# Linear attention in a two-layer trunk: the gate projection r as four pairs in seven block products, and head outputs with tokens on partitions

## The chip, the cores and the metric

The kernel runs on one core of one Trainium2 chip. The metric is the device time of one execution in microseconds, the median of the runs shown. Matrix products run on TensorE (PE in the profile, its weight loads PEld), elementwise work on VectorE (DVE) and ScalarE (ACT), and POOL (GpSimd) issues the DMAs that add into their destination. SP issues nearly all other loads.

## The reference

The program is a trunk of two layers over 512 tokens of width 1024, all in float32. Layer 0 mixes by pooling and short convolution, layer 1 by gated linear attention (GLA); each is followed by a gated ConvFFN of width 2816. The change lies in layer 1's mixer, which reads the normed input hn = rmsnorm(x) through one projection, split into q, k (512 columns each), v, r (1024 each) and a gate of rank 16:

```python
q, k, v, r, gl = jnp.split(hn @ gla_w_in, ...)
g = jax.nn.log_sigmoid(gl @ w_g2 + b_g) / 16
# four heads, chunks of 64 tokens; bcum = cumsum of g in a chunk
att = where(mask, (q * exp(bcum)) @ (k * exp(-bcum)).T, 0)
o = att @ v + (q * exp(bcum)) @ state
state = exp(b_last) * state + (k * exp(b_last - bcum)).T @ v
o = o * lax.rsqrt(jnp.mean(o * o, axis=-1, keepdims=True) + EPS) * norm_g   # per head, 256 wide
y = (o * silu(r)) @ gla_w_out
```

## The kernel before

Activations lie with channels on partitions: a tile is 128 channels by 512 tokens. The input norm is put off: the projections work on x times the norm's gain, and their results are multiplied afterwards by rs, the factor per token spread over the partitions (y4 holds the same factors with tokens on partitions). For precision every product is done in three: weights and activations are each split into a high and a low part (`hi` is a copy on ScalarE in the rounded format fp32r, `lo` the difference, on VectorE), and hi x hi, hi x lo and lo x hi are summed in PSUM. Products of the attention itself run in plain fp32.

The q/k projection of a head is not done as two plain tiles but as one pair of tiles in seven block products, a scheme of Strassen's kind: of the 2 x 2 blocks of weights (left and right tile, two halves of the contraction) and of activations (`mixed`, sums of x's halves in tokens and channels), seven products of half width, 12 matmuls of 256 columns each, stand for eight. `seven_weights` makes the sums of weights: `load_sum` loads two quarters, `add_sum` adds two others to them by a DMA on POOL's queue (the tile s31), `load_left` and `load_right` bring three quarters of the rest, and `s2_sum` and `s4_sum` form the other sums on VectorE; all are then split in high and low (L484, L490). `keep`, `add_p5` and the last sum put the result together from the banks stx, styz and stz.

The r projection is eight plain tiles, `gate(i)`: 24 matmuls of 512 columns each (L1324), scaled by rs (L370), then Silu. Their weights come through the same queue of blocks as the plain tiles of other stages, `weight_order`, with one load (L218) and one split (L223, L227) a tile.

A head goes through `keys` and `keys2` (q and k times the decays), `scores` (att, and the transposes kot of the keys), `kv`, `states`, and `outputs`. `outputs` makes o with channels on partitions: two banks of 128 channels by 512 tokens, 14 matmuls with 128 result columns. The norm of o is then a sum over partitions: squares on ScalarE (L1215), added, split, and summed by two matmuls with ones (`totals`, L315 and L316, the tile ss), followed by the chain of `norm_wide` on 128x512 tiles; `scale` multiplies o by the result ro and the norm's gain (L1235), and `out_gate` by silu(r), and splits the product into y_h and y_l for the output projection `go`.

From layer 1's projection to the end of the r tiles each step has a planned time by hand: `at(t, fn)` puts a step at t, `then(us, fn)` also moves t on by what TensorE needs, and `run_plan` sorts all steps by time and fixes that order on PE, DVE and ACT. An engine works through its own list in that order; a step that has to wait holds up those behind it on its engine. DMA queues likewise issue in order. Banks of PSUM (eight) and tiles of SBUF come from pools, and a new user waits for the old one's last reader.

The order of the attention stage is written out: r tile, q/k pair, r tile, q/k pair and so on, the steps of the heads set in between, and from the fifth r tile on r alone. Ahead of it, the value and gate projection runs in four blocks of columns (vg), with the gate's logits (`gate_logits`, the tile z) of heads 0 and 1 after the second block and of heads 2 and 3 within the third.

Of the kernel before, what the change touches and what calls it, by code (L numbers as in the profile page):

```python
# [73 lines left out]
def trunk_kernel(ctx, tc, xT, cols, w_ab, w_pool, w_abo, w_vg, w_qk, w_r, w_g2, w_go, w_up, w_dn, w_ds, outT):  # L74
# [109 lines left out]
    def weight_order():  # L184
# [7 lines left out]
        for l in range(2):  # L192
            for j, k0, kt in down_blocks():
                yield w_dn[l, j, :, k0 * P : (k0 + kt) * P], kt, P, SKEW * (l == 1 and j == KD - 1)
            if l == 0:
                off = 0
                for n, ks in zip(VG_COLS, VG_K):
                    for kt in ks:
                        yield w_vg[:, off : off + kt * n], kt, n, VG_SKEW
                        off += kt * n  # L200
                for i in range(8):
                    yield w_r[i], KD, P
                for j in TILE_ORDER:
                    yield w_go[j], KD, P
# [251 lines left out]
    def seven_weights(src, base, pool, sums, behind=False, lead=None, later=0.0):  # L456
# [50 lines left out]
        at(base - 26.0, queued_sum if behind else load_sum)  # L507
        at(base - 20.0, add_sum)
# [12 lines left out]
        at(base - (18.0 if lead == 0 else 15.4), load_left)  # L521
        at(base - (13.0 if lead == 0 else 9.7), load_right)
        for n, (t, step) in enumerate(zip(when, steps)):
            at(base + t + ((0, 0, 1.2, 1.2, 0.6, 0.6)[lead or 0] if 3 <= n <= 6 else later if n == 0 else 0.0), step)
# [510 lines left out]
    y4 = sp.tile([P, NTT], F32, tag="y4", name="y4")  # L1035
    rs = slot(name="rs")
# [159 lines left out]
    def outputs(h):  # L1196
        q = heads[h]
        att = att_t[h % 2]
        q["o"] = []
        for e in range(2):  # L1200
            o = bank("o")
            for p in range(NTT):
                cs = slice(p * P, (p + 1) * P)
                PE.matmul(o[:, cs], vcols(p, h * 256 + e * P, P), att[:, cs], start=True, stop=p == 0)
                if p:
                    PE.matmul(o[:, cs], q["st"][p][:, e * P : (e + 1) * P], q["q2"][:, cs], start=False, stop=True)
            q["o"].append(o)

    def squares_of(h, t):
        q = heads[h]  # L1210

        def raw():
            q["sq"] = [slot(name="osq") for _ in range(2)]
            for sq, o in zip(q["sq"], q["o"]):
                S.activation(sq, o, AF.Square)  # L1215

        def total():
            V.tensor_tensor(q["sq"][0], q["sq"][0], q["sq"][1], ALU.add)
            q["ro"], q["norm"] = norm_wide(q["sq"][0], 256, "ro")

        at(t, raw)
        at(t + (0.6 if h == 3 else 1.3), total)
        ready_at = (6.5, 6.5, 1.7, 0.8)[h]
        at(t + ready_at, lambda: q["norm"][0]())
        at(t + ready_at + (1.6 if h < 2 else 0.6), lambda: q["norm"][1]())

    def out_norm(h, t):
        q = heads[h]
        late = 13.0 if h == 0 else 0.0
        for step, after in zip(range(3, 8), (0.0, 0.7, 1.4, 2.2, 3.0 + late)):  # L1230
            at(t + after, lambda step=step: q["norm"][step]())

        def scale(e):
            q.setdefault("y", []).append(slot(name="y"))
            V.scalar_tensor_tensor(q["y"][e], q["o"][e], col("gnorm", e), q["ro"], ALU.mult, ALU.mult)  # L1235

        for e in range(2):
            at(t + 3.8 + late + 0.7 * e, lambda e=e: scale(e))

    def out_gate(h, e, t):  # L1240
        i = 2 * h + e

        def gate():
            y = heads[h]["y"][e]
            V.tensor_tensor(y, y, sil[i], ALU.mult)

        def high():
            y_h[i] = slot(F32R, "yh")
            S.activation(y_h[i], heads[h]["y"][e], AF.Copy)

        def low():
            y_l[i] = slot(F32R, "yl")
            V.tensor_tensor(y_l[i], heads[h]["y"][e], f32(y_h[i]), ALU.subtract)
# [33 lines left out]
    for b, (n, ks) in enumerate(zip(VG_COLS, VG_K)):  # L1287
        k0 = 0
        for i, kt in enumerate(ks):
# [14 lines left out]
            if b == 2 and i == 0:  # L1304
                for h in range(HEADS):
                    at(t + 2.2 + 0.1 * h, lambda h=h: log_gate(h))
                    at(t + 4.6 + 0.1 * h, lambda h=h: log_gate2(h))
                    if h < 2:
                        at(t + 6.0 + 2.0 * h, lambda h=h: log_gate3(h))
# [3 lines left out]
    scaled_at, sil_at = {}, {}  # L1313

    def project_into(name, key, store, between, split_at):
        q = {}

        def part(i):
            if i == 0:
                q["o"] = (bank(name), *ready.pop(0))  # L1320
            o, h, lo = q["o"]
            w, a = ((h, xh), (h, xl), (lo, xh))[i // 2]
            for k in (k1, k2)[i % 2]:
                PE.matmul(o, w[:, k, :], a[k], start=i == 0 and k == 0, stop=k == KD - 1 and i == 5, skip_group_check=True)  # L1324

        def out():
            store(key, scaled(q["o"][0], rs, name))

        next_block(13.0, *split_at)
        for i in range(6):  # L1330
            then(HK * MM, lambda i=i: part(i))
            if i in between:
                between[i]()
        at(t + (-0.8 if key == 7 else 0.3), out)

    qk_ops = {}

    def queries_keys(h):
        nonlocal t
        w = seven_weights(w_qk[h], t, "gla", 2)  # L1340
        b, q = {}, {}

        def product(name):
            if not qk_ops:
                qk_ops.update(operands(mixed))
# [5 lines left out]
            seven_product(w, b, qk_ops, name, out, first, ts)  # L1351
# [13 lines left out]
        def query():  # L1365
            V.tensor_tensor(q["q"], b["yz"], q["q"], ALU.add)

        def query2():
            V.tensor_tensor(q["q"], q["q"], rs, ALU.mult)
            heads[h]["q"] = q["q"]  # L1370

        for n, name in enumerate(DOWN_SEVEN):
            at(t + n * UNIT, lambda name=name: product(name))
        at(t + 1 * UNIT + 0.1, lambda: keep("q", lo_t))
        at(t + 3 * UNIT + 0.1, lambda: keep("q", hi_t))
        at(t + 4 * UNIT + 0.2, lambda: add_p5("q"))
        at(t + 5 * UNIT + 0.1, lambda: keep("k", hi_t))
        at(t + 5 * UNIT + 0.6, lambda: add_p5("k"))
        t += 7 * UNIT
        at(t - 0.6, query)  # L1380
        at(t + 0.1, lambda: keep("k", lo_t))
        at(t + 0.15, query2)
        at(t + 0.8, key)

    def store_r(i, u):
        sil[i] = u

    def gate(i, between={}, split_at=(6.0, 4.8)):
        project_into("r", i, store_r, between, split_at)
        at(t + 1.2, lambda: S.activation(sil[i], sil[i], AF.Silu))  # L1390
        sil_at[i] = t + 1.8
# [201 lines left out]
```

## Time and profile before

| | |
|---|---|
| median of 3 runs | 1006.9 us (1006.19, 1006.9, 1437.49) |
| profiled execution: span, first to last instruction | 1005.9 us |
| profiled execution's time by the median: span and what lies around it | 1005.9 + 1.0 us |
| TensorE busy in the span | 995.5 us (99%) |
| VectorE, ScalarE, POOL busy | 851.1 (85%), 616.1 (61%), 81.3 (8%) us |
| TensorE in the chain that ended last | 90% |
| attention stage, from the first r matmul to the first matmul of `go` | 513.84 to 625.07 us |
| HBM read | 145.35 MB, 147 GB/s over the span |

The page's first part is busy time by engine, the fourth the chain of work that ended last, followed back from the end. A matmul's busy time runs from its start to its modelled end, so matmuls that follow each other overlap: the distance between starts tells the pace, and the chain gives it. A group's row shows count, busy time, mean ns of one, and the idle time before them with what ended it.

### The profile page before, as it was taken

To read this page: it belongs to the slowest core of one execution; us is meant where nothing else is said; L and a number is where in the kernel's file an instruction comes from. 1 tells how busy PE (TensorE), PEld (TensorE's weight loads), DVE (VectorE), ACT (ScalarE), POOL (GpSimd) and SP (SyncE) were. 2 spreads that over 40 slices of the span, in tenths; PEclk is the share of its full clock that TensorE was granted. 3 is DMA by queue.
4 is the path that set the end of the run, shared out by engine and by line. 5 is a ranking of instruction groups with operands and counts; after the bars stand their busy time and mean duration, and the time that the engine had idled before them with its cause. 6 is when DMAs were issued, how large, how long until landed. Compare 5 with 4: busy or idle time off the path is not lost.

```text
span 1005.9 us, 17757 instructions
## 1 busy us (share of the span) xinstructions
PE 995.5 (99%) x7070; PEld 927.9 (92%) x7070; DVE 851.1 (85%) x1241; ACT 616.1 (61%) x959; POOL 81.3 (8%) x105
## 2 busy tenths in 40 slices
PE   9999999999999999999999999999999999999996
PEld 7888889999999988899999998889999999988896
DVE  7886689999999997768768787889999999997775
ACT  6442467667666754345775777667676676754451
POOL 0000211111111000002000000111101101000000
PEclk9999999999999999999999999999999999999998
DMA  6533757788787454527325122677888777454522
GB/s 220 154 102 105 179 125 171 207 201 196 197 205 189 128 127 136 137 81 206 99 82 140 53 75 87 183 170 167 211 209 197 187 204 190 130 124 141 128 85 84
DMA packets 64083, 151.22 MB, mean 150 GB/s; under 512 B 5408, under 2 KB 8352, under 8 KB 64000
## 3 DMA queue, kind: packets, MB, share of 16 engines
q1 hardware_dynamic: 46640, 117.46, 37.7%
q0 software_dynamic: 16672, 31.99, 19.2%
q8 instruction: 55, 0.90, 0.4%
q10 hardware_dynamic: 688, 0.65, 0.2%
q14 instruction: 28, 0.23, 0.1%
HBM read 145.35 MB, written 2.10 MB: 147 GB/s over the span
## 4 chain that ended last, share of the span: by engine, by line
PE 90%; DVE 4%; ACT 2%; DMA 2%; issue 1%; DVEq 0%; ACTq 0%
PE stx L538 28%; PE styz L538 16%; PE dn L268 15%; PE go L268 4%; PE abo L268 4%; PE r L1324 3%; PE pc L268 2%; PE dn L538 2%; PE pb L268 2%; PE px L268 2%; PE stz L538 2%; PE vg L1112 1%; PE vg L1113 1%; PE vg L1114 1%; PE pu L268 1%
## 5 line engine op out<-in xcount | busy, mean ns | idle before, releaser
L490 DVE TENSOR_TENSOR lo<-raw,hi 128x1024 fp32r<-128x1024 f32 x112 | 136.7, 1220 | 14.1 <-ACT hi L484 13.8
L484 ACT ACTIVATE hi<-raw 128x1024 fp32r<-128x1024 f32 x112 | 117.8, 1057 | 31.9 <-DMA raw<-in_w_up 10.7
L227 DVE TENSOR_TENSOR lo<-raw,hi 128x1024 fp32r<-128x1024 f32 (+3 forms) x79 | 91.1, 1154 | 18.1 <-ACT hi L223 17.9
L466 POOL DMA_DIRECT2D s<-in_w_up x44 | 53.1, 1206 | 533.8 <-ACT yh L177 97.8
L223 ACT ACTIVATE hi<-raw 128x1024 fp32r<-128x1024 f32 (+3 forms) x79 | 78.7, 997 | 13.0 <-issue 3.9
L359 DVE SCALAR_TENSOR_TENSOR cacc<-u,colt,cacc 128x511 f32<-128x511 f32 x96 | 71.5, 744 | 3.9 <-ACT cacc L356 3.8
L356 ACT ACTIVATE cacc<-u,colt 128x512 f32<-128x512 f32 x48 | 39.2, 817 | 49.8 <-DVE u L660 40.2
L490 DVE TENSOR_TENSOR lo<-s,hi 128x1024 fp32r<-128x1024 f32 x56 | 68.2, 1217 | 0.0
L538 PE MATMUL stx<-th,hi 128*128 128x256 f32 x384 | 59.6, 277 | 0.2 <-ACT kk L645 0.2
L484 ACT ACTIVATE hi<-s 128x1024 fp32r<-128x1024 f32 x56 | 59.0, 1053 | 0.8
L538 PE MATMUL stx<-tl,hi 128*128 128x256 f32 x384 | 59.2, 276 | 0.0
L538 PE MATMUL stx<-th,lo 128*128 128x256 f32 x384 | 59.2, 276 | 0.0
L538 PE MATMUL styz<-xh,hi 128*128 128x256 f32 x368 | 56.9, 277 | 0.0
L538 PE MATMUL styz<-xh,lo 128*128 128x256 f32 x368 | 56.7, 276 | 0.0
L538 PE MATMUL styz<-xl,hi 128*128 128x256 f32 x368 | 56.7, 276 | 0.0
L268 PE MATMUL dn<-mh,hi 128*128 128x512 f32 (+1 forms) x238 | 56.5, 377 | 0.0
L268 PE MATMUL dn<-mh,lo 128*128 128x512 f32 (+1 forms) x238 | 56.4, 376 | 0.0
L268 PE MATMUL dn<-ml,hi 128*128 128x512 f32 (+1 forms) x238 | 56.4, 376 | 0.0
L538 PEld LDWEIGHTS stx<-th,hi 128*128 128x128 f32 x384 | 50.7, 188 | 0.7 <-ACT kk L645 0.4
L538 PEld LDWEIGHTS stx<-tl,hi 128*128 128x128 f32 x384 | 50.7, 188 | 0.0
L538 PEld LDWEIGHTS stx<-th,lo 128*128 128x128 f32 x384 | 50.7, 188 | 0.0
L268 PEld LDWEIGHTS dn<-mh,lo 128*128 128x128 f32 x238 | 42.9, 188 | 8.2
(334 smaller groups left out, 2583.2 us busy)
## 6 DMA issues: line engine op xcount, KB each, us to landing
s<-in_w_up SPq DMA_DIRECT2D x44, 512.0 KB, 6.9
s<-in_w_up POOLq DMA_DIRECT2D x44, 512.0 KB, 7.2
raw<-in_w_up SPq DMA_DIRECT2D x44, 512.0 KB, 6.7
raw<-in_w_dn SPq DMA_DIRECT2D x32, 448.0 KB, 3.4
raw<-in_w_up SPq DMA_DIRECT2D x44, 256.0 KB, 3.4
raw<-in_w_ab SPq DMA_DIRECT2D x14, 512.0 KB, 3.7
raw<-in_w_abo SPq DMA_DIRECT2D x8, 512.0 KB, 3.6
s<-in_w_ds SPq DMA_DIRECT2D x8, 512.0 KB, 6.5
```

The costliest lines, as they stand in the source:

```text
L223: S.activation(parts[0], raw, AF.Copy)
L227: V.tensor_tensor(parts[1], raw, f32(parts[0]), ALU.subtract)
L268: PE.matmul(out, w[:, k, :], a[k], start=first and i == 0 and k == 0, stop=last and i == 2 and k == n - 1, skip_group_check=loose,)
L356: S.activation(acc[0], u, AF.Identity, bias=col(bname, j), scale=col(wname, 2 * nj + j))
L359: V.scalar_tensor_tensor(a, u[:, : T - i], col(wname, (2 - i) * nj + j), a, ALU.mult, ALU.add)
L466: G.dma_start(w["s31"].rearrange("p (a n) -> p a n", a=2), part, accum_op=ALU.add)
L484: S.activation(h, src(), AF.Copy)
L490: V.tensor_tensor(lo, src(), f32(h), ALU.subtract)
L538: PE.matmul(b[out][:, ts], wt[:, ks[k]], a[k], start=first and i == 0 and k == 0, stop=i == 2 and k == HK - 1, skip_group_check=True,)
L1112: PE.matmul(o[c][:, :n], xh[kk][:, cs], h[:, k, :], start=kk == 0, stop=False)
L1113: PE.matmul(o[c][:, :n], xl[kk][:, cs], h[:, k, :], start=False, stop=False)
L1324: PE.matmul(o, w[:, k, :], a[k], start=i == 0 and k == 0, stop=k == KD - 1 and i == 5, skip_group_check=True)
```

## The change

The r projection is done in four pairs of tiles in seven block products, by the same code as q and k (`pair` takes the place of `queries_keys`, and of `gate` with `project_into`). The four q/k pairs now stand first, one after the other, and the four r pairs behind them, with the steps of the heads in between. The weights of r are laid out in pairs in memory.

A head's output is made with tokens on partitions: four pieces of 128 tokens by 256 channels, seven matmuls, with the roles of weights and data exchanged. Its mean square is then a sum along the row, which ScalarE's Square gives beside its result (`accum_out`); the root is taken on 128x4 tiles, ScalarE scales the pieces, and eight transposes on TensorE (`rows`) bring them back to channels on partitions for the gating, which now reads the bank directly.

q and k are no longer multiplied by rs: k's factor, with its sign, is put into v (y4n = -y4 * y4), and q's into the norm of the output. All four heads' gate logits stand after vg's second block, and the steps that follow them stand earlier. `seven_weights` can start loads (`begin`) and splits (`early`) at other times.

```diff
-                for i in range(8):
-                    yield w_r[i], KD, P
...
-    def seven_weights(src, base, pool, sums, behind=False, lead=None, later=0.0):
+    def seven_weights(src, base, pool, sums, behind=False, lead=None, later=0.0, begin=(26.0, 20.0, 15.4, 9.7), early=0.0):
...
-        at(base - 26.0, queued_sum if behind else load_sum)
-        at(base - 20.0, add_sum)
+        at(base - begin[0], queued_sum if behind else load_sum)
+        at(base - begin[1], add_sum)
...
         if pool == "gla":
-            when = (*when[:7], 4.4, 1.5, 5.3)
+            when = (-6.75, -4.35, -2.1, -1.6, -0.9, -0.2, 0.5, 4.4, 1.5, 5.3)
...
     def v_out(b, n, c):
         o = v_banks[b][c]
-        S.activation(vcols(c, b * 256, 256), o[:, :256], AF.Copy, scale=y4[:, c : c + 1])
+        S.activation(vcols(c, b * 256, 256), o[:, :256], AF.Copy, scale=y4n[:, c : c + 1])
...
     def outputs(h):
         q = heads[h]
         att = att_t[h % 2]
-        q["o"] = []
+        two = [bank("o") for _ in range(2)]
+        q["o"] = [two[p // 2][:, p % 2 * 256 : p % 2 * 256 + 256] for p in range(NTT)]
+        for p in range(NTT):
+            cs = slice(p * P, (p + 1) * P)
+            PE.matmul(q["o"][p], att[:, cs], vcols(p, h * 256, 256), start=True, stop=p == 0)
+            if p:
+                PE.matmul(q["o"][p], q["q2"][:, cs], q["st"][p], start=False, stop=True)
+
+    def out_norm(h, t, root=2.2):
+        q = heads[h]
+        small = {}
+
+        def squares():
+            two = [slot(name="ot") for _ in range(2)]
+            q["ot"] = [two[p // 2][:, p % 2 * 256 : p % 2 * 256 + 256] for p in range(NTT)]
+            small["s"] = sp.tile([P, NTT], F32, tag="os", name="os")
+            for p in range(NTT):
+                S.activation(
+                    q["ot"][p], q["o"][p], AF.Square, scale=y4[:, p : p + 1], accum_out=small["s"][:, p : p + 1]
+                )
+
+        def mean():
+            small["v"] = sp.tile([P, NTT], F32, tag="v4", name="v")
+            V.tensor_scalar(small["v"], small["s"], 1.0 / 256, EPS, ALU.mult, ALU.add)
+
+        def seed():
+            small["y"] = sp.tile([P, NTT], F32, tag="oy", name="oy")
+            S.activation(small["y"], small["s"], AF.Abs_reciprocal_sqrt, bias=eps_t, scale=1.0 / 256)
+
+        def factor():
+            r = sp.tile([P, NTT], F32, tag="t4", name="t")
+            f = q["f"] = sp.tile([P, NTT], F32, tag="of", name="of")
+            V.tensor_tensor(r, small["y"], small["v"], ALU.mult)
+            V.scalar_tensor_tensor(r, r, -0.5, small["y"], ALU.mult, ALU.mult)
+            V.scalar_tensor_tensor(r, r, 1.5, small["y"], ALU.add, ALU.mult)
+            V.tensor_tensor(f, r, y4, ALU.mult)
+
+        def scale():
+            for p in range(NTT):
+                S.activation(q["ot"][p], q["o"][p], AF.Copy, scale=q["f"][:, p : p + 1])
...
+    def rows(h):
+        q = heads[h]
+        q["yt"] = [bank("yt") for _ in range(2)]
         for e in range(2):
-            o = bank("o")
             for p in range(NTT):
-                cs = slice(p * P, (p + 1) * P)
-                PE.matmul(o[:, cs], vcols(p, h * 256 + e * P, P), att[:, cs], start=True, stop=p == 0)
-                if p:
-                    PE.matmul(o[:, cs], q["st"][p][:, e * P : (e + 1) * P], q["q2"][:, cs], start=False, stop=True)
-            q["o"].append(o)
-
-    def squares_of(h, t):
...
+                PE.transpose(q["yt"][e][:, p * P : (p + 1) * P], q["ot"][p][:, e * P : (e + 1) * P], ident)
...
         def gate():
-            y = heads[h]["y"][e]
-            V.tensor_tensor(y, y, sil[i], ALU.mult)
+            V.scalar_tensor_tensor(sil[i], heads[h]["yt"][e], col("gnorm", e), sil[i], ALU.mult, ALU.mult)
...
                 then(0.9, lambda: rsqrt_small(y4, sums(acc)[:, :NTT], NTT, D))
+                at(t + 2.0, lambda: V.scalar_tensor_tensor(y4n, y4, -1.0, y4, ALU.mult, ALU.mult))
...
-            if (b, i) in ((1, 1), (2, 0)):
-                for h in ((0, 1) if b == 1 else (2, 3)):
+            if (b, i) == (1, 1):
+                for h in range(HEADS):
                     then(0.24, lambda h=h: gate_logits(h))
                     at(t + 1.5, lambda h=h: gate_sizes(h))
...
+                    at(t + 3.4 - 0.1 * h, lambda h=h: log_gate(h))
+                    at(t + 5.8 - 0.1 * h, lambda h=h: log_gate2(h))
+                for h in range(3):
+                    at(t + 7.2 + 2.2 * h, lambda h=h: log_gate3(h))
...
-    def queries_keys(h):
+    def pair(src, kind, h, between=None, early=0.0, begin=(26.0, 20.0, 15.4, 9.7)):
...
-        def key():
-            V.scalar_tensor_tensor(q["k"], q["k"], -1.0, rs, ALU.mult, ALU.mult)
...
-        def query2():
-            V.tensor_tensor(q["q"], q["q"], rs, ALU.mult)
...
+        def left_scaled():
+            V.tensor_tensor(q["r"], q["r"], rs, ALU.mult)
+
+        def right_scaled():
+            V.scalar_tensor_tensor(q["n"], q["n"], -1.0, rs, ALU.mult, ALU.mult)
+
+        def silu(i, tile):
+            sil[2 * h + i] = q[tile]
+            S.activation(q[tile], q[tile], AF.Silu)
...
-    gate(0)
-    gates_of(0, t)
-    at(t + 4.9, lambda: log_gate3(2))
-    queries_keys(0)
-    head_keys(0, 1.6)
-    gate(1, {4: lambda: head_scores(0)}, (3.6, 2.4))
...
-    gate(5, {4: lambda: (head_kv(3), head_norm(2))})
-    gate(6, {1: lambda: head_out(3)})
-    gate(7, {1: lambda: head_norm(3)}, (10.0, 8.6))
...
+    pair(w_qk, "qk", 0)
+    head_keys(0, 0.2)
+    gates_of(1, t - 4.0)
+    at(t + 4.0, lambda: log_gate3(3))
+    pair(w_qk, "qk", 1)
+    head_keys(1, 0.2)
+    gates_of(2, t - 3.0)
+    head_scores(0)
+    pair(w_qk, "qk", 2, {3: (lambda: head_kv(0),)}, 1.6, (17.5, 12.5, 13.5, 9.0))
+    head_keys(2, 0.2)
+    gates_of(3, t - 5.0)
+    head_out(0, 4.5)
+    head_scores(1)
+    pair(w_qk, "qk", 3, {3: (lambda: head_kv(1),)}, 4.6)
+    head_keys(3, 0.2)
+    head_out(1)
+    head_scores(2)
+    pair(w_r, "r", 0, {3: (lambda: head_kv(2),)}, 4.6)
+    head_out(2)
+    head_scores(3)
+    pair(w_r, "r", 1, {3: (lambda: head_kv(3),), 5: (lambda: head_rows(0),)}, 4.6)
+    head_gates(0, -1.0)
+    head_out(3, 5.5)
+    pair(w_r, "r", 2, {3: (lambda: head_rows(1),)}, 2.5)
+    head_gates(1, -1.0)
+    pair(w_r, "r", 3, {2: (lambda: head_rows(2),), 5: (lambda: head_rows(3),)}, 0.0, (17.5, 12.5, 13.5, 9.0))
+    head_gates(2, -1.0)
+    head_gates(3, 3.0)
     for i in range(2):
-        block(t - 9.5 + 2.5 * i, t - 6.5 + 2.0 * i, t - 4.8 + 2.0 * i)
+        block(t - 9.5 + 2.5 * i, t - 4.5 + 2.0 * i, t - 2.8 + 2.0 * i)
...
-        "w_r": _blocks(gw[:, 2048:3072], P),
+        "w_r": _blocks(gw[:, 2048:3072], P).reshape(HEADS, 2, P, D).transpose(0, 2, 1, 3).reshape(HEADS, P, 2 * D),
```

More of the change, by code (lines that the diff above doesn't have):

```diff
@@ L1035, in trunk_kernel @@
     y4 = sp.tile([P, NTT], F32, tag="y4", name="y4")
+    y4n = sp.tile([P, NTT], F32, tag="y4n", name="y4n", bufs=1)
     rs = slot(name="rs")
@@ L1209, in squares_of @@
-    def squares_of(h, t):
[L1210 to L1238, printed above, removed]
+                PE.transpose(q["yt"][e][:, p * P : (p + 1) * P], q["ot"][p][:, e * P : (e + 1) * P], ident)
@@ L1310, in trunk_kernel @@
         for c in range(NTT):
             at(t + 0.1 + 0.4 * c, lambda b=b, n=n, c=c: v_out(b, n, c))
[L1313 to L1334, printed above, removed]
@@ L1350, in product @@
             }[name]
-            seven_product(w, b, qk_ops, name, out, first, ts)
+            seven_product(w, b, pair_ops, name, out, first, ts)
         def keep(tile, ts):
@@ L1374, in queries_keys, with left_sum @@
[L1374 to L1391, printed above, removed]
+        def left_sum():
+            V.tensor_tensor(q[left], b["yz"], q[left], ALU.add)
+            if kind == "qk":
+                heads[h]["q"] = q["q"]
@@ new lines, in right_done @@
+        def right_done():
+            heads[h]["k"] = q["k"]
+        def left_scaled():
[5 more added lines that the diff above has]
+            S.activation(q[tile], q[tile], AF.Silu)
+        for n, name in enumerate(DOWN_SEVEN):
+            for step in (between or {}).get(n, ()):
+                step()
+            starts_at.append(t)
+            then(UNIT, lambda name=name: product(name))
@@ L1393, in head_keys @@
     def head_keys(h, d=0.0):
         at(t + d, lambda: keys(h))
-        at(t + d + 2.6, lambda: keys2(h))
+        at(t + d + 2.4, lambda: keys2(h))
     def head_scores(h):
@@ L1402, in head_kv, with head_out, head_rows @@
     def head_kv(h):
-        then(1.0, lambda: kv(h))
+        then(1.3, lambda: kv(h))
         at(t + 0.1, lambda: states(h))
-    def head_out(h):
-        then(3.1, lambda: outputs(h))
-        squares_of(h, t + 0.1)
-    def head_norm(h):
-        then(0.46, lambda: heads[h]["norm"][2]())
-        out_norm(h, t + 0.1)
-        scaled_at[h] = t + 5.4
+    def head_out(h, root=2.2):
+        then(3.0, lambda: outputs(h))
+        out_norm(h, t + 0.1, root)
+    def head_rows(h):
+        then(0.9, lambda: rows(h))
     def gates_of(h, t):
```

75 lines of the change are left out of this document (34 added, 41 removed).

## The prediction, written before the changed kernel ran

> **What bounds the kernel now.** I read the page first: who is busy, and on which engine the chain that ended last lies.
>
> ```profile
> span 1005.9 us, 17757 instructions
> PE 995.5 (99%) x7070; PEld 927.9 (92%) x7070; DVE 851.1 (85%) x1241; ACT 616.1 (61%) x959; POOL 81.3 (8%) x105
> PE 90%; DVE 4%; ACT 2%; DMA 2%; issue 1%; DVEq 0%; ACTq 0%
> ```
>
> TensorE bounds it, but a "busy" PE here holds the time in which a matmul stood waiting too, so 99% is no proof of pace. Next the busy time of the attention stage, cut where the chain changes tiles: from the end of the value and gate projection (vg) to the first matmul of the output projection (go). The columns are the stretch, its length, the busy time of TensorE, its weight loads, VectorE, ScalarE and POOL with instruction counts, granted clock, DMA share and GB/s.
>
> ```profile
> 513.84:625.07 111.23, 110.97 (x749) 101.30 (x749) 88.01 (x147) 76.16 (x113) 2.44 (x2) 1.00 0.31 88
> ```
>
> The change lies here: 111.23 us, clock 1.00, VectorE 79% and ScalarE 68% busy, the DMA engines 31%. Pace is read from the chain in order of time, whose second column is how long a run of matmuls held the array.
>
> ```profile
> 513.84 5.45 PE r L1324 x24
> 519.29 1.38 PE stx L538 x12
> ...
> 528.83 4.56 PE r L1324 x20
> 533.38 0.89 PE att L1159 x8
> 534.27 0.84 PE att L1163 x8
> 535.12 0.34 PE kot L1167 x3
> ...
> 546.01 1.29 PE kv L1184 x6
> 547.30 4.58 PE r L1324 x20
> 551.88 0.44 PE o L1204 x4
> ...
> 555.01 0.89 PE att L1159 x8
> ...
> 567.78 0.23 PE ss L315
> 568.01 0.23 PE ss L316
> ...
> 620.88 0.50 PE ss L316
> 621.38 3.69 PE r L1324 x16
> 625.07 4.99 PE go L268 x22
> ```
>
> A plain r tile takes 5.45; a q/k pair in seven products 528.83 - 519.29 = 9.54; scores of a head 0.89 + 0.84 + 0.34 = 2.07; kv 1.29; a head's output 555.01 - 551.88 = 3.13; the two matmuls that sum its squares 0.46. The stage holds 8 x 5.45 + 4 x (9.54 + 2.07 + 1.29 + 3.13 + 0.46) = 43.60 + 65.96 = 109.56 us of work. It lasts 625.07 - 513.84 = 111.23, so 1.67 us of stall is all that better hiding could give; the rest must come from doing less on TensorE.
>
> **The change part by part, TensorE first.** Four r pairs in seven products replace eight plain tiles: they run the same loop on the same shapes as the q/k pairs, so 4 x 9.54 = 38.16 for 43.60: -5.44. The two matmuls of the squares go, 4 x 0.46: -1.84. A head's output is now seven matmuls with a 128x256 result and 128 rows of contraction, which is the shape of kv (three logical ones in 1.29, 0.43 each): 3.01 for 3.13, over four heads -0.48. New are eight 128x128 transposes a head, as in kot (three in 0.34, 0.113 each): 0.91, over four heads +3.63. The sum is -4.13, nearly all on the bounding engine.
>
> The transposes are the one price with two readings, for the group row gives each a far longer duration than its share of the chain:
>
> ```profile
> L1167 PE MATMUL kot<-ident,kb 128*128 128x128 f32 x12 | 2.0, 275 | 0.0
> ```
>
> 275 ns is start to end of one, 113 the distance between two that stand behind each other. Eight stand in a row in the new code, more than the three of kot, so I take 113; the other end is 275, which adds 32 x 0.162 = 5.2. The Trainium skill (TensorE: Matmul & The Clock Gate, Part 4: PE-mode transpose) speaks against the change here: in its words the clock gate's full rate "doesn't engage" for transposes, and it measured about 275 ns for one in a kernel. By that figure, an estimate from the page, the sum would be some 5 us worse. The trace agrees with its 275 as a duration, but shows a granted clock of 1.00 in this stage and the shorter distance.
>
> **Stalls.** Of the old ones the rows show the norm's at the end (ss at 620.88 took 0.50 for its 0.23); that chain goes. Between a head's keys and its scores lay part of a plain tile, 4.56, and now lies a whole pair, 9.54. So I drop the 1.67, and look for new ones. Three places can stall anew.
>
> First, all four gate-logit matmuls (z) stand together in the vg stage, and the next vg block takes its four banks from them, each when VectorE has read it:
>
> ```profile
> 491.12 0.47 PE z L1058 x2
> 491.39 1.41 DVE L1060 TENSOR_SCALAR z<-z,colt 128x512 f32<-128x512 f32 x2 [1.35 <-PE z L1058]
> ```
>
> One z is read 0.27 + 0.70 = 0.97 after its start; TensorE is through all four after 0.94. The later banks are asked for 12 matmuls apart, a quarter of the 5.5 that four such runs take (a vg block has as many columns as an r tile, 5.45), and two 128x512 passes (0.68 each, by the L1245 row below) stand between the second and third read: third bank free 0.27 + 3 x 0.70 + 1.36 = 3.73 after the first start, asked for at 0.94 + 0.3 + 2 x 1.36 = 4.0. 0.3 us of stall; 0 to 1.4, if those passes came first.
>
> Second, the weights of r. A plain tile needed one load and one split; a pair needs two loads, a sum made by a load and an adding DMA on POOL's queue, three wide splits and one narrow one. By the landings in this stretch:
>
> ```profile
> s<-in_w_qk SPq DMA_DIRECT2D x4, 512.0 KB, 5.2
> s<-in_w_qk POOLq DMA_DIRECT2D x4, 512.0 KB, 9.0
> ```
>
> load, then add: 5.2 + 9.0 = 14.2 us. The plan starts them 26 us ahead of most pairs, but 17.5 ahead of the third q/k pair and the last r pair; there the sum is first used some 5 us into the pair, after 2.3 of splitting, so 17.5 + 2.7 = 20.2 are there. SP issues in order, and each load waits for a buffer of three; a pair's last split is 6.5 us after its start, and the load that waits for it is planned after that. POOL has only these adds in the stage. I cost this at nothing; it is covered by 6 us, and without the cover costs what is missing, twice. Moved bytes rise by 4 x (1.75 - 1.0) = 3 MB, under a DMA share of 0.31.
>
> Third, the end: go's first part reads all of heads 0 to 2, and head 2's last split waits on ScalarE behind the copy of the last product. 0.38 + 0.63 (rows below) is 1.01 after the last r product; go reads it as its sixth matmul, 5 x 0.227 = 1.14 after. Head 3 is first read 8.2 us in. I take 0.4, 0 to 0.9. With 0.2 for copies between products as in the stx rows above (1.38 for 1.36), new stalls are 0.9.
>
> **VectorE and ScalarE**, which have to keep up:
>
> ```profile
> L227 DVE TENSOR_TENSOR lo<-raw,hi 128x1024 fp32r<-128x1024 f32 x9 | 11.0, 1218 | 1.4 <-ACT hi L223 1.4
> L1245 DVE TENSOR_TENSOR y<-y,r 128x512 f32<-128x512 f32 x8 | 5.2, 683 | 0.0
> L1235 DVE SCALAR_TENSOR_TENSOR y<-o,colt,ro 128x512 f32<-128x512 f32 x8 | 5.7, 746 | 0.1
> L1359 DVE TENSOR_TENSOR q<-stz,q 128x256 f32<-128x256 f32 x4 | 1.7, 416 | 0.0
> L223 ACT ACTIVATE hi<-raw 128x1024 fp32r<-128x1024 f32 x10 | 10.5, 1048 | 0.0
> L1078 DVE TENSOR_TENSOR_SCAN bc<-starts,z 128x512 f32<-128x512 f32 x2 | 2.4, 1224 | 0.1
> L1390 ACT ACT_TABLE_LOAD x7 | 9.0, 1283 | 0.1
> L1356 ACT ACTIVATE k<-stx 128x256 f32<-128x256 f32 x8 | 3.0, 379 | 6.0 <-PE stx L538 6.0
> L1249 ACT ACTIVATE yh<-y 128x512 fp32r<-128x512 f32 x8 | 5.0, 632 | 4.3 <-DVE y L1245 4.3
> ```
>
> VectorE, per head: gone are six 128x512 passes (four of the wide norm, the two by rs on q and k, now that y4n = -y4 squared sits in v), two scalings by ro, two products with r, two wide splits: 6 x 0.68 + 2 x 0.75 + 2 x 0.68 + 2 x 1.22 = 9.4. New: three wide splits, one narrow, two sums of weights, two adds of p5, the left sum, two gating passes out of PSUM, five of 128x4 (no row here; under 0.42 each, I take 0.16): 3.66 + 2.05 + 0.83 + 0.68 + 1.49 + 0.8 = 9.5. So 88 stays 88 in some 106 us, 83%. ScalarE, per head: gone two wide copies, six norm passes of about 0.63, 5.9; new three wide and one narrow copy, four copies of products, eight 128x256 passes at 0.47 and a seed of 0.3, 9.3. The Square that also sums its row has no row: between 0.38 (a 128x256 copy out of PSUM) and 0.63 (twice as wide) I take 0.47, nearer the first; off the path. Table loads, 1.28 each, go from 16 to 7 by the order of the instructions (-11.5), so ScalarE does 76 + 13.6 - 11.5 = 78 us. Both have room, and cost nothing while waits between them stay as they are.
>
> **Sum.** -4.13 - 1.67 + 0.9 = -4.9: span 1001.0. The profiled execution's span is 1005.9 and the median of the runs 1006.9, so 1.0 lies around it: 1002.0 us.
>
> **The rivals.** (a) VectorE binds the r pairs. It idles 111.23 - 88.01 = 23.2 us in the stage now; if none of that can be squeezed, it needs 88 + 23 = 111, less 1.22 + 0.68 of head 2's scan and the pass before it, moved to vg: a stage of 109 where the forecast has 106.3, so 1002.0 + 2.9 = 1004.9. For: each r pair alternates high and low four times where two tiles did it twice. Against: the norm's alternations go, and splits are planned up to 4.6 us earlier. (b) Slower than before: the transposes do not overlap, so that each of the 32 holds the array for its 275 ns: 1002.0 + 5.2 = 1007.2. It decides from 0.113 + 4.9 / 32 = 0.266 us each. For: the duration in the kot group row, and they come eight at a time. Against: the kot row in the chain. (The Trainium skill, TensorE: Matmul & The Clock Gate, Part 4: PE-mode transpose, would lead one to expect this.) (c) The sum of the weights comes late in both short-lead pairs. At the longest landings seen on these tiles, 9.2 + 12.4 = 21.6 against 20.2: 1.4 twice, 1004.8.
>
> ```profile
> DMA to landing us min/median/max: 4.7/5.5/9.2
> DMA to landing us min/median/max: 6.2/9.3/12.4
> ```
>
> (Loads from SP, then adds from POOL.) (d) It does not do what it says: TensorE saves 4.1 and gives it all back in waits, 1006 to 1007.
>
> **How the numbers follow.** Forecast 0.73 (1000.8 to 1003.5), (a) 0.12, (b) 0.04, (c) 0.05, (d) 0.04, better than forecast 0.02. If every stall went, 1006.9 - 4.13 - 1.67 = 1001.1, and two of the three times shown lie 0.7 apart, so the low end is 1000.4. The high end takes in (a) and (c) with 0.7 more, 1005.6; (b) and (d) are left out. A 2% bound, about what a measurement of this kernel can tell from no change, is 20 us: four times all that the stage can give, and four times the dearest lateness priced above. Faster 0.01, same 0.97, slower 0.02.
>
> **What would show it.** Right: in the changed profile go starts near 620.2, r pairs step 9.54 in the chain, eight yt transposes hold 0.9, the waits name no PE stall over 0.5, seven table loads. Wrong: stx or stz runs of the r pairs that take 2 us or more for 1.36 (a or c, told apart by whether lo or a DMA released them), or yt runs of 2.2 (b).

## The result and the profile after

The changed kernel takes 1023.2 us (median of 4 runs, 1022.8 to 1023.7) where the kernel before took 1007.7 on the same chip: 1.0159 of it by the means, 95% interval 1.0143 to 1.0175, so slower by 1.6% where the forecast was 1002.0 us, 0.5% faster. (One run of the kernel before took 1437 us and is left out of the ratio.) The page of the changed kernel:

```profile
span 1021.8 us, 18084 instructions
PE 1010.0 (99%) x7182; PEld 947.4 (93%) x7182; DVE 852.3 (83%) x1258; ACT 619.1 (61%) x1003; POOL 86.2 (8%) x109
PE 95%; DVE 3%; ACT 1%; DMA 0%; issue 0%; DVEq 0%; SPq 0%; ACTq 0%
```

TensorE carries the chain even more than before (95% for 90%), though its work was forecast to fall. So cut the span where TensorE changes its work: at the first vg matmul, the first matmul behind vg, the first of `go`. The columns are those of the stage row in the prediction; first the kernel before, then the changed one. (The first matmul of `go` starts at 624.91; the chain's row at 625.07 stands 0.16 behind it.)

```profile
0.00:465.80 465.80, 464.38 (x3134) 426.65 (x3135) 396.86 (x564) 270.87 (x424) 37.46 (x57) 1.00 0.61 159
465.80:513.84 48.04, 48.04 (x410) 47.85 (x409) 35.73 (x59) 34.40 (x57) 5.67 (x15) 1.00 0.45 126
513.84:624.91 111.07, 110.81 (x749) 101.14 (x748) 87.85 (x147) 76.00 (x113) 2.44 (x2) 1.00 0.31 88
624.91:1005.90 380.99, 372.23 (x2781) 352.27 (x2779) 330.67 (x474) 234.81 (x366) 35.73 (x31) 0.99 0.63 162
```

```profile
0.00:474.17 474.17, 472.80 (x3135) 434.11 (x3135) 397.35 (x564) 272.02 (x424) 37.46 (x57) 1.00 0.60 156
474.17:523.44 49.27, 49.12 (x411) 48.60 (x410) 39.06 (x65) 36.71 (x60) 5.80 (x15) 1.00 0.42 123
523.44:632.45 109.01, 107.65 (x862) 104.93 (x860) 86.28 (x159) 77.14 (x155) 7.25 (x6) 1.00 0.51 124
632.45:1021.80 389.35, 380.39 (x2782) 359.76 (x2780) 329.64 (x472) 233.24 (x364) 35.73 (x31) 0.99 0.61 157
```

The attention stage is 2.1 us shorter. The loss lies where no instruction was changed: 8.4 us in layer 0, before the edit is reached, and 8.4 us from `go` on, with the same counts of matmuls and the same granted clock. Nor is it waits: outside vg and the attention stage the list of waits names 3.9 us on TensorE before and 3.5 after. It is the pace. The chain in layer 0's up-projection, before and after:

```profile
201.94 2.72 PE styz L538 x24
204.66 2.72 PE stx L538 x24
207.38 1.36 PE styz L538 x12
```

```profile
196.67 2.72 PE stx L536 x24
199.39 1.36 PE styz L536 x12
200.75 2.78 PE stx L536 x24
203.53 2.88 PE styz L536 x24
206.41 2.88 PE stx L536 x24
```

Twenty-four matmuls of 256 columns hold the array for 2.72 us, 113 ns each, before; for 2.72 to 2.88, up to 120 ns each, after. The switch shows in the timeline of the changed kernel (start, time to the modelled end of the last, four matmuls a row):

```profile
201.50 0.62 PE L536 MATMUL stx<-th,lo 128*128 128x256 f32 x4
201.95 0.64 PE L536 MATMUL stx<-th,sh 128*128 128x256 f32 x4
202.43 0.63 PE L536 MATMUL stx<-tl,sh 128*128 128x256 f32 x4
202.90 0.63 PE L536 MATMUL stx<-th,sl 128*128 128x256 f32 x4
203.37 0.65 PE L536 MATMUL styz<-xh,hi 128*128 128x256 f32 x4
...
204.33 0.64 PE L536 MATMUL styz<-xh,lo 128*128 128x256 f32 x4
...
212.95 0.64 PE L536 MATMUL stx<-th,sl 128*128 128x256 f32 x4
213.43 0.62 PE L536 MATMUL styz<-xh,hi 128*128 128x256 f32 x4
213.88 0.62 PE L536 MATMUL styz<-xl,hi 128*128 128x256 f32 x4
```

Read the starts: 0.45 a row until 201.95, then 0.47 to 0.48 from the product on sh and sl on. These are the narrow weight tiles of product p6, the only weights of the seven products that lie in a stage's own pool and not with the wide tiles hi and lo. In the up-projection the pace changes by turns: behind one p6 it stays slow, and within the next, here at 213, it goes back to 0.45, with no gap on TensorE in between and a granted clock of 1.00 from 195 to 201 and from 203.4 to 212.5 alike. Of all 5,104 distances under 200 ns from a 256-column matmul of the seven products or of `dn` to the next matmul in the changed kernel 56% are 116 ns or more, 3% of 4,774 before; the surplus over 113.4 ns adds up to 17.9 us and 0.5 us. That is the loss of 15.9 us in span, and more.

What moved is an address. The change adds seven new small buffers to the pool of small tiles (y4n, and two each of os, oy and of), 32 bytes a partition each. The pools of the stages lie behind it, and by the allocation of the two built programs they start at byte 204128 instead of 203904: 224 bytes on, no longer a multiple of 128. sh and sl start 76 bytes into their buffers (`SKEW`, 19 elements), as the wide tiles do, and the activations that the seven products read start at multiples of 128. So the narrow weights' address, less that of the data that runs past them, went from 76 to 44 modulo 128, and that of the wide tiles kept 76. "Difference" means this number below. One more thing moved with the pools: some tiles mh and ml, the data of `dn`. Of its plain matmuls (512 columns, weights at a multiple of 128) 135 went from a difference of 0 to 32, and 17 of 256 columns from 76 to 108.

### The profile page after: what moved, and what is told of

Same layout as the page of the kernel before. It is cut to its first block, busy times and chain, and to the rows that moved or that the text cites. A ratio compares the mean times of both kernels' runs of the same rounds, so it can differ in the third digit from the quotient of the medians.

```text
span 1021.8 us, 18084 instructions
## 1 busy us (share of the span) xinstructions
PE 1010.0 (99%) x7182; PEld 947.4 (93%) x7182; DVE 852.3 (83%) x1258; ACT 619.1 (61%) x1003; POOL 86.2 (8%) x109
## 4 chain that ended last, share of the span: by engine, by line
PE 95%; DVE 3%; ACT 1%; DMA 0%; issue 0%; DVEq 0%; SPq 0%; ACTq 0%
PE stx L536 32%; PE styz L536 19%; PE dn L266 15%; PE abo L266 4%; PE go L266 4%; PE dn L536 2%; PE pc L266 2%; PE pb L266 2%; PE px L266 2%; PE stz L536 2%; PE vg L1111 2%; PE vg L1113 1%; PE vg L1112 1%; PE pu L901 1%; PE pu L266 1%; PE o L1202 1%
## 5 line engine op out<-in xcount | busy, mean ns | idle before, releaser
L488 DVE TENSOR_TENSOR lo<-raw,hi 128x1024 fp32r<-128x1024 f32 x120 | 146.3, 1220 | 21.6 <-ACT hi L482 21.4
L482 ACT ACTIVATE hi<-raw 128x1024 fp32r<-128x1024 f32 x120 | 125.3, 1056 | 24.5 <-PE styz L536 14.6
L225 DVE TENSOR_TENSOR lo<-raw,hi 128x1024 fp32r<-128x1024 f32 (+3 forms) x71 | 81.6, 1151 | 11.0 <-ACT hi L221 11.0
L221 ACT ACTIVATE hi<-raw 128x1024 fp32r<-128x1024 f32 (+3 forms) x71 | 70.2, 990 | 14.3 <-DMA raw<-in_w_ab 4.1
L536 PE MATMUL stx<-th,lo 128*128 128x256 f32 x416 | 65.3, 279 | 0.0
L536 PE MATMUL stx<-tl,hi 128*128 128x256 f32 x416 | 65.3, 279 | 0.0
L536 PE MATMUL styz<-xh,hi 128*128 128x256 f32 x400 | 63.2, 280 | 0.0
L536 PE MATMUL styz<-xh,lo 128*128 128x256 f32 x400 | 63.0, 279 | 0.2 <-DVE lo L488 0.2
L536 PE MATMUL styz<-xl,hi 128*128 128x256 f32 x400 | 62.8, 279 | 0.0
L536 PEld LDWEIGHTS styz<-xh,lo 128*128 128x128 f32 x400 | 53.7, 188 | 0.4 <-DVE lo L488 0.4
```

Source lines behind the costliest of these rows:

```text
L221: S.activation(parts[0], raw, AF.Copy)
L225: V.tensor_tensor(parts[1], raw, f32(parts[0]), ALU.subtract)
L482: S.activation(h, src(), AF.Copy)
L488: V.tensor_tensor(lo, src(), f32(h), ALU.subtract)
L536: PE.matmul(b[out][:, ts], wt[:, ks[k]], a[k], start=first and i == 0 and k == 0, stop=i == 2 and k == HK - 1, skip_group_check=True,)
```

## The experiments

"Pitch" is the mean distance between the starts of consecutive 256-column matmuls of the seven products and of `dn`, from the timelines. Addresses are those of the built programs.

| kernel | difference, wide / narrow | pitch, wide / narrow, ns | median, us |
|---|---|---|---|
| before | 76 / 76 | 113.5 / 113.6 | 1007.0 to 1007.7 |
| changed | 76 / 44 | 116.7 / 118.1 | 1023.2 |
| changed, spacer + 32 bytes | 76 / 76 | 113.8 / 113.6 | 1007.0 |
| before, spacer + 32 bytes | 76 / 108 | 113.6 / 119.8 | 1012.8 |
| changed, narrow offset 27 | 76 / 76 | 114.0 / 113.8 | 1008.2 |
| before, narrow offset 27 | 76 / 108 | 113.6 / 119.7 | 1011.4 |
| before, narrow offset 11 | 76 / 44 | 116.9 / 118.1 | 1023.0 |
| changed, narrow offset 35 | 76 / 108 | 113.9 / 119.6 | 1012.4 |
| before, all offsets 27 | 108 / 108 | 120.1 / 120.1 | 1037.3 |
| before, all offsets 35 | 12 / 12 | 119.8 / 119.7 | 1036.1 |

**The change with the old addresses.**

```diff
-    sp.tile([P, 48], F32, tag="gap", name="gap", bufs=1)
+    sp.tile([P, 56], F32, tag="gap", name="gap", bufs=1)
```

> The changed kernel with its spacer tile in the pool of small tiles 32 bytes per partition longer, so that the tiles of every stage start at a multiple of 64 bytes again, as they did before the change; nothing else differs. Theory A (the change's seven small tiles moved the stage tiles, the narrow weight tiles sh and sl among them, to 32 bytes off a multiple of 64, and that makes half of all 256-column products run at 120 ns a matmul instead of 113): all products return to 113 to 114 ns; some 5,600 matmuls of 256 columns with about 3.3 ns less each are 18.5 us, so the span falls from 1021.8 to about 1003 and the time to 1004 to 1006. Rival B (the new order of instructions, the tile allocation in PSUM or the load of the other engines slows the products; addresses play no part): 1022 to 1024 as without the spacer, with the mix of 113 and 120 ns unchanged.

1007.0 us (1005.5 to 1008.1, 11 runs), 0.9993 of the kernel before (0.9984 to 1.0002). Rival B falls: the whole loss goes with 32 bytes, and no instruction differs. The sum was 17.9 us over 5,104 distances, not 18.5 over 5,600. The time lies 1 us above the range, for a reason taken up below.

**The old kernel with the new kind of address,** the same edit in the kernel before:

> The kernel before, with only its spacer tile 32 bytes per partition longer: the stage tiles start 32 bytes off a multiple of 64, as after the change, and no instruction differs. Theory A (addresses of the stage tiles): half of the 256-column matmuls at 120 ns, 5,500 matmuls by 3.3 ns, so about 1007 + 18 = 1025 (1018 to 1027). Rival B (instruction order): 1006 to 1008, all products at 113 ns.

1012.8 us, 1.0054 (1.0040 to 1.0068). A loss with no instruction changed, as theory A has it, but 5.6 us and not 18, below theory A's range: sh and sl run at 119.8, the wide weights stay at 113.6. Either the changed kernel's own stream spreads the slow pace (rival C), or 32 bytes up and 32 down are not alike.

**The narrow weights alone,** in the changed kernel and in the one before:

```diff
-[:, SKEW : SKEW + T]
+[:, SKEW + 8 : SKEW + 8 + T]
```

> The changed kernel; only the offset of the narrow weight tiles sh and sl inside their own buffers goes from 19 to 27 elements (32 bytes), so that the addresses that the matmuls read their weights from lie 12 bytes behind a multiple of 64 like those of all the wide weight tiles; the buffers themselves, and the tiles s31, mh and ml of the same pools, stay 32 bytes off. Theory A1 (what counts is the address of the narrow weights): 1004 to 1008. Theory A2 (what counts is another tile of the stage pools, or the DMAs and VectorE reads on them): 1020 to 1024. Rival B (instruction order): 1022 to 1024.

> The kernel before; only the offset of the narrow weight tiles sh and sl inside their buffers goes from 19 to 27 elements (32 bytes), so that they alone lie at 44 instead of 12 bytes behind a multiple of 64. Theory A1 (address of the narrow weights): 1018 to 1027, with half of all 256-column matmuls at 120 ns, those on wide weights among them. Theory A2 (other tiles of the stage) and rival B (instruction order): 1006 to 1008.

1008.2 us (1.0004 of before; 0.9987 to 1.0020) and 1011.4 us (1.0039; 1.0024 to 1.0054). So the address of the narrow weights decides (A1); moving the other tiles of the stage too cost another 1.4 us at most, 1012.8 for 1011.4. The traces put 1.2 of it on `dn`: its 630 plain matmuls, 135 of which read the moved mh and ml, step 228.9 ns with the longer spacer and 227.0 with the offset alone. The first of these two runs lies 0.2 above its range (the 135 still stand at 32 there, at 234.5 ns, 1.0 us); the second missed its number by far, as the run before it did.

**Up and down.** Eight elements less in the kernel before, sixteen more in the changed one:

> The kernel before; only the offset of the narrow weight tiles sh and sl in their buffers goes from 19 to 11 elements, so that they lie 32 bytes below (not above, as in the run at 27 elements, which read 1011.4 us) the residue that they share with all the wide weight tiles: the same residue modulo 256 as in the changed kernel as it stood. Theory A (the address alone decides, and this residue lets the slow pitch run on through the products behind p6): half of all 256-column matmuls at 120 ns, 1007 + 18 = 1025 (1021 to 1027). Rival C (the slow pitch runs on only in the changed kernel's own instruction stream; a shift of 32 bytes in either direction costs the same): 1010 to 1013, wide-weight products at 113.4 ns.

> The changed kernel without the longer spacer; the offset of sh and sl goes from 19 to 35 elements, so that they lie 32 bytes above the residue of the wide weight tiles instead of 32 bytes below. Theory A (address alone): sh and sl products at 118.6 ns, those on wide weights back near 113.4, so some 3 to 5 us above the run of this kernel at the wide tiles' residue (1007 to 1008): 1010 to 1013. Rival C (the changed stream makes the slow pitch run on): 1021 to 1024, as without the edit.

1023.0 us (1.0153; 1.0139 to 1.0166) and 1012.4 us (1.0045; 1.0032 to 1.0059). Rival C falls: the kernel before, with one constant changed, shows the changed kernel's whole loss and the same chain,

```profile
199.84 2.78 PE stx L538 x24
202.62 2.88 PE styz L538 x24
205.50 2.88 PE stx L538 x24
```

and the changed kernel with a difference of 108 loses next to nothing behind p6 (113.9 on the wide weights).

**All weights together.** `SKEW = 27`, then 35, in the kernel before:

> The kernel before; the offset goes from 19 to 27 elements in the wide and the narrow weight tiles of the seven-product blocks alike, so that all of them move by 32 bytes together and share one residue again. Theory A-relative (what costs is that the weights change their residue from one product to the next): 1006 to 1008, all at 113.4 ns. Theory A-absolute (this residue is slow by itself, 118.6 ns wherever it stands): 5,400 matmuls by 5.2 ns, 1007 + 28 = 1035 (1030 to 1037).

> The kernel before; the offset in the wide and the narrow weight tiles of the seven-product blocks goes from 19 to 35 elements, so that all of them move by 64 bytes together (27 elements, 32 bytes, read 1037.3 us). Theory A64 (the weights' address counts modulo 64 bytes): 1006 to 1009, all products at 113.4 ns. Theory A128 (it counts modulo 128 or more): another value, somewhere between 1007 and 1045, with most products off 113.4 ns.

1037.3 and 1036.1 us (1.0294; 1.0280 to 1.0308, and 1.0288; 1.0273 to 1.0304). That the weights share one place does not help (A-relative falls), and 64 bytes are no period: 12 and 76 differ. The first run lies 0.3 above A-absolute's range, for each matmul lost 6.7 ns and not 5.2. In both runs every piece of the chain is of this kind (the run at 27):

```profile
201.87 2.88 PE stx L538 x24
204.75 2.88 PE styz L538 x24
```

**Weights against data.** The spacer among the constants moves weights and the activations th and tl by 32 bytes, but not xh and xl, which lie ahead of it:

```diff
-    cp.tile([P, 40], F32, tag="gap", name="gap")
+    cp.tile([P, 48], F32, tag="gap", name="gap")
```

> The kernel before; the spacer tile in the pool of constants 32 bytes per partition longer. It moves every tile behind it by 32 bytes: the weight tiles and the activations th, tl, bh, bl, mh and ml, but not xh and xl, which lie ahead of it. Theory W (the weights' own address counts): as with all weight tiles moved alone, 1035 to 1039, products of th and of xh alike at 119 ns. Theory R (the weights' address against that of the moving operand counts): products of th and tl back at 113.4 ns, those of xh and xl at 119; some 1,700 of the 5,400 matmuls read xh or xl, 1,700 by 5.5 ns = 9 us, so 1014 to 1020.

1031.6 us (1.0246; 1.0229 to 1.0263). The timeline tells the two apart within one product pair:

```profile
202.18 0.65 PE L538 MATMUL styz<-xh,lo 128*128 128x256 f32 x4
202.67 0.64 PE L538 MATMUL stx<-th,hi 128*128 128x256 f32 x4
203.15 0.63 PE L538 MATMUL stx<-tl,hi 128*128 128x256 f32 x4
203.61 0.62 PE L538 MATMUL stx<-th,lo 128*128 128x256 f32 x4
204.07 0.62 PE L538 MATMUL stx<-th,sh 128*128 128x256 f32 x4
```

Products on xh and xl step 0.49 a row; those on th and tl, on the same wide weights hi and lo, fall back to 0.45 or 0.46 within a few matmuls. On average xh and xl read 121.8 ns, the others 115.1. By kind of row theory R holds and W falls: it is the difference of the two addresses. R's number was too low: 2,112 matmuls read xh and xl and not 1,700, each lost 8.4 ns and not 5.5, and the others lost 1.7 ns behind them. Two groups outside the seven products bear it out. In this run 563 plain matmuls of 512 columns read xh or xl at a difference of 32 instead of 0 and step 233.3 ns, where those still at 0 step 226.9. And in the changed kernel the 135 of `dn`, whose data moved while their weights stayed at a multiple of 128, step 233.7, where the 495 others step 227.2; with the spacer all 630 step 227.0.

**The rest of the gain.** The changed kernel with the longer spacer and four shifts in its plan:

```diff
-    head_keys(0, 0.2)
+    head_keys(0, 1.8)
...
-            at(t + 1.0, lambda: silu(0, left))
+            at(t + 1.0 + (1.2 if h < 3 else 0.0), lambda: silu(0, left))
...
-    head_out(0, 4.5)
+    head_out(0, 6.0)
...
-    pair(w_r, "r", 1, {3: (lambda: head_kv(3),), 5: (lambda: head_rows(0),)}, 4.6)
-    head_gates(0, -1.0)
+    pair(w_r, "r", 1, {3: (lambda: head_kv(3),)}, 4.6)
+    head_rows(0)
+    head_rows(1)
+    head_gates(0, 0.3)
+    head_gates(1, 3.6)
...
-    pair(w_r, "r", 2, {3: (lambda: head_rows(1),)}, 2.5)
-    head_gates(1, -1.0)
+    pair(w_r, "r", 2, None, 2.5)
```

(The second silu moves like the first.)

> The changed kernel with the spacer of 32 bytes and four shifts in the plan of the attention stage: head 0's keys after the low half of the first weight sum (a wait of 0.6 us on it), the output scaling of head 0 1.5 us later and the r tiles' SiLU 1.2 us later, but for the last pair (two waits of 0.6 and 0.4 us on ScalarE's copies out of PSUM), and the transposes of heads 0 and 1 ahead of head 3's output products, so that no seven-block product follows them directly (93 matmuls at 120 instead of 113.4 ns, 0.6 us). Theory D (the rest of the expected gain went to these waits and to slow stretches behind the transposes): 1.5 to 2.2 us less than with the spacer alone, 1004.8 to 1005.7 beside 1007.0. Rival E (the waits move on to the next engine, or the transposes' banks hold up the next pair): 1006.5 to 1009.

1005.8 us (1004.9 to 1006.8, 11 runs), 0.9982 of the kernel before (0.9973 to 0.9991): the only version whose interval lies below the kernel before, by 0.2%. It is 1.3 us below the run with the spacer alone, less than the 1.5 to 2.2 of theory D, and part of that is rival E's doing. The wait on the low half of a wide weight sum of the second q/k pair, which stands behind head 0's keys on VectorE, fell from 0.74 to 0.24 us, that on q's copy went, but the one on r's copy came again a pair earlier:

```profile
600.69 1.82 ACT ot L1215 x8
602.51 0.52 ACT yh L1260
603.03 0.28 ACT r L1345
603.35 1.65 PE stx L536 x12
```

Twelve matmuls in 1.65 for 1.36: eight passes on heads' outputs and the split yh, which the moved transposes let start sooner, now stand ahead of r's copy on ScalarE.

How much of the 1.3 us the shifts made isn't shown. Of the 1.5 us between the two profiled spans 0.8 lies in the attention stage and another 0.8 in vg (48.44 us for 49.28), while the stretches around them nearly cancel. vg lost its slow pace though no shift touches it, and with the narrow offset 27 and the unshifted plan it has none either. Nor is the fall from 0.74 to 0.24 shown to be the shift's doing: with the narrow offset 27 and the unshifted plan that wait was 0.13. In both of these runs the first pair ran slow, 1.44 a product, and TensorE came later to the weights.

## Why the prediction was wrong, point by point

**What failed is its frame:** it summed the attention stage with its two edges, vg and the start of `go`, and put the rest of the kernel at nothing, since no instruction there is edited. Its list of what the change adds names y4n and the passes on 128x4 tiles, but costs them only in VectorE time. The new tiles' 224 bytes moved every stage's tiles. The surplus over 113.4 ns between two 256-column matmuls, vg's counted too, is 7.9 us up to vg, 0.9 in vg, 1.6 in the attention stage and 8.2 behind it: 18.6 in all, of which 2.2 stay when the addresses are put back. The 135 plain matmuls of `dn` lost another 0.9. The bound by which 2% was out of reach, four times all that the stage can give, was drawn around the stage too.

**With the old addresses the stage can be judged by itself.** The changed kernel with the longer spacer:

```profile
0.00:466.11 466.11, 464.36 (x3134) 426.87 (x3135) 397.27 (x564) 271.46 (x424) 37.47 (x57) 1.00 0.60 158
466.11:515.39 49.28, 49.13 (x411) 48.60 (x410) 39.11 (x65) 36.76 (x60) 5.56 (x15) 1.00 0.42 122
515.39:624.09 108.70, 107.19 (x860) 104.47 (x860) 86.44 (x159) 77.22 (x155) 7.25 (x6) 1.00 0.51 124
624.09:1005.60 381.51, 372.71 (x2782) 352.29 (x2780) 329.31 (x472) 232.12 (x364) 35.73 (x31) 0.99 0.62 160
```

Span 1005.6, forecast 1001.0: of the 4.9 us expected, 0.3 came. Its chain gives the terms:

```profile
548.30 0.86 PE o L1202 x4
...
550.88 0.43 PE o L1204 x2
551.32 0.89 PE att L1158 x8
...
555.22 1.28 ACT L1225
556.51 0.30 ACT oy L1225
556.81 1.90 ACT hi L482 x2
558.71 1.45 ACT ot L1237 x4
...
560.44 0.28 ACT q L1345
...
594.37 0.87 PE yt L1250 x8
595.25 1.44 PE styz L536 x12
596.69 1.44 PE stx L536 x12
```

- *TensorE, -4.13: right.* Products of the r pairs take 1.36 where nothing slows them, eight transposes 0.87 for the 0.91 forecast, an output 3.02 (548.30 to 551.32) for 3.01. The stage's work is thus 109.56 - 4.13 = 105.43 as summed; with waits of 1.9 and a surplus pitch of 1.1 it comes to 108.4 of the 108.70 measured.
- *Old stalls, -1.67: right.* The norm's wait is gone, and none of the stage's waits is an old one.
- *New stalls in the stage, forecast 0.2 for copies: wrong, 1.9.* The list of waits, TensorE's in the stage:

```profile
PE styz L536 <- DVE lo L488: 0.6, 1, 0.6
PE stx L536 <- ACT q L1345: 0.6, 1, 0.6
PE stx L536 <- ACT r L1345: 0.4, 1, 0.4
```

  By the starts around them they cost 0.74, 0.73 and 0.44: a wide split of the second q/k pair on VectorE came late, and twice ScalarE's copy out of PSUM. The chain shows the second: a table load, the seed, two wide copies and four scalings stood ahead of q's copy, all of it work that the prediction had put "off the path" because ScalarE as a whole has room (it forecast 78 us, the stage shows 77.22). A share of busy time does not show who stands ahead in the order.
- *Pace behind the new work, not foreseen: 1.9.* 0.85 in vg behind the four z together, 1.1 in the stage, mostly after yt: the two products after 594.37 take 1.44. With the narrow difference back at 76 such stretches stand behind yt in all three kernels that have it (spacer, narrow offset 27, shifted plan), at the stage's first pair in two of them, and in vg in one. What starts one was not tried by itself, so that the new work makes them is not shown.
- *z, forecast 0.3, and the tail at go, forecast 0.4: right.* vg is 1.24 longer, 0.85 of it pitch; go loses 0.5 within its first 13 matmuls (its 192 hold 44.04 us for 43.52).
- *Loads of r's weights, costed at nothing: right.* TensorE waits on no DMA in the stage, though POOL does 7.25 us there for 2.44. VectorE 86.44 for 88; six table loads in the stage and one 4.8 us behind it, the seven of the forecast.

By stretch, the 4.6 between 1005.6 and the forecast are 0.3 in layer 0, 0.9 in vg (1.24 less the 0.3), 3.2 in the stage and 0.1 behind it, with 0.1 of rounding; of the stage's 3.2, 1.7 are waits, 1.1 pace, and 0.4 isn't assigned.

**The rivals.** (a), (b) and (c) fall: one wait of 0.6 on VectorE in the stage, no transposes at 275 ns, no late sum. The Trainium skill (TensorE: Matmul & The Clock Gate, Part 4: PE-mode transpose) gives about 275 ns for a transpose in a kernel; here the duration of one is again like that, 273, while eight take 0.87. (d), all given back in waits, 1006 to 1007, had 0.04. Once the addresses are put right its number comes, 1007.0, but its mechanism only in part: of some 5.5 us given back 1.9 are waits in the stage and 1.9 slow pace. More than 2% slower had 0.02, and 1.6% stays inside that bound; but no rival came near 1023, and none had a place outside the stage and its edges.

## What to carry to other kernels

A small buffer added to a pool moves what is allocated behind it: before a change is costed, compare the addresses of both builds, and where a loss shows in code that nobody edited, compare pitch (starts, not modelled durations: the group rows' means differ by 1%, 276 and 279 ns) before looking for waits. Put the old addresses back with a spacer and judge the change only then. And where a step is "off the path", look at who stands behind it in the order of its engine, not at the engine's share.

## What the runs showed of the hardware

A 128x256 matmul in fp32r follows the last after 113.4 ns or after some 120, at a granted clock of 1.00, by where its weights start relative to the data that runs past them. By this difference modulo 128, 76 bytes gave 113.5 to 114.0 on average (115.1 in the run where it changed places with 108 from product to product); 108 gave 119.6 to 120.1 (121.8 in that run); 12 gave 119.7 to 119.8. Plain matmuls of 512 columns stepped 226.9 to 227.7 at 0, 233.3 to 234.5 at 32, and 229.8 at 96. From 0 to 32 they lose about as much as those of 256 columns do from 76 to 108, 6.5 ns, so the price is one a matmul and not one a column.

At 44, tried on the narrow weights in both kernels, these ran at 118.1, and the slow pace went on over half the matmuls behind them, whose own difference was 76; at 108 it did not. So the pace is also a state that outlives its cause. In the up-projection one p6 started it and the next ended it, by turns, with no gap on TensorE; in the attention stage slow stretches also stand where every difference of the seven products is 76. What sets and ends the state is open. No difference was tried that is not a multiple of 32 away from 0 or 76, a period above 128 is not excluded, and why it is so these runs don't show.

The Trainium skill (SBUF — State Buffer, Operand start alignment) asks only for a multiple of the element size, and says that this is "about legality, not speed"; here the speed of two legal addresses differs by 6%.
